# A two-layer encoder step on one core: the order in which weights are split, one last quarter instead of two halves, and two groups of moved work

## The chip, the cores and the metric

The kernel runs on one core of one Trainium2 chip. Its time is device microseconds (us) of one execution; the figure of a kernel is the median of its runs. Five engines work side by side, each in the order of its own queue: TensorE (PE in the profile; PEld is its weight load), VectorE (DVE), ScalarE (ACT), GpSimd (POOL), and SyncE (SP), which here only starts DMAs.

## What is computed

One inference step of a small encoder for two request groups: a prompt of 1024 columns and 32 new columns of another stream, so T = 1056 columns of D = 1024. Layer A mixes with an mLSTM recurrence, layer B with windowed attention whose keys and values are shared; each is followed by a SwiGLU feed-forward (D_FF = 2816), and each of the four sub-layers by a LayerNorm of `alpha * x + sublayer(x)`. All of it is float32.

```
def trunk(x, ...):
    for layer in range(DEPTH):                       # DEPTH = 2
        if layer < N_A_LAYERS:
            mix, C, n, m = mlstm_mixer(x, w_in_a[layer], ..., w_out_a[layer], C0s[layer], n0s[layer], m0s[layer])
        else:
            if layer == N_A_LAYERS:
                kv = (x @ w_kv).reshape(B, T, 2, N_KV_HEADS, HEAD_DIM)
            mix = swa_prompt(...) if k_cache is None else swa_sample(...)   # window 128, sinks, ALiBi
        x = layer_norm(DEEPNORM_ALPHA * x + mix, ln_g[layer, 0], ln_b[layer, 0])
        x = layer_norm(DEEPNORM_ALPHA * x + swiglu(x, w_gu[layer], w_down[layer]), ln_g[layer, 1], ln_b[layer, 1])
    return x, jnp.stack(Cs), jnp.stack(ns), jnp.stack(ms), k_sh, v_sh

def swiglu(x, w_gu, w_down):
    g, u = jnp.split(x @ w_gu, 2, axis=-1)
    return (jax.nn.silu(g) * u) @ w_down
```

The outputs are the final x of both groups, the recurrent states, and the new rows of keys and values.

## The kernel before

**Products.** Every float32 product is made of three: a number is split into a high part `h` and a rest `l`, and TensorE adds h·h, h·l and l·h (`gemm`, L344 to L346, one line each). The columns are worked through in groups of 384, 384, 288 for projections and in quarters of 264 for everything else. Activations lie in `ACT`, their halves in `SX`.

**Weights.** Weights come from memory as float32 "units" of 128 x 1024 (`Weights`). `load_to` starts a unit's DMA into one of RAW = 3 buffers `wr` (queue of SyncE). `_next` splits the next half unit: the high part is a copy on ACT (L190), the rest a subtraction on POOL, or on DVE for the keys in `on_vector` (L192). The results lie in one of SLOTS = 5 pairs of buffers `wh`/`wl`, or in a place of their own (`home`: the tiles `ex` and `oh`). Feed-forward units come in pairs and give seven factors, some of them sums made on DVE. `get` and `factor` split what is missing at the place of use; `done` frees a unit's buffers and then splits on, until four slots are taken or the next unit is twelve or more ahead.

**The order of the work.** No scheduler moves instructions: each engine gets them in the order in which the program writes them. What is written when is set by `Weave`. It holds generators ("tasks": mLSTM, LayerNorm, staging, attention); `gemm` calls `tick` after each of its steps with the model time of three matmuls, 3 · (n/2400 + 0.003) us, n at least 256, and each task whose pause has run out writes its next instructions. The numbers in `LN_PACE` and after `yield` are such pauses. They aren't times of the chip.

**Stages, in time** (us of the profiled execution): loading and first projections (0 to 65); mLSTM beside the projections of q, k, v and the output gate (65 to 415); layer A's output projection, with LayerNorm (415 to 535); feed-forward of layer A: two plain tiles for each half of the columns (to 590), 20 up tiles in pairs with seven factors (to 1000), down blocks, and a last part in quarters (to 1250); keys, values, queries and attention (to 1530); layer B's output projection (to 1590) and feed-forward (plain tiles to 1675, up tiles to 2085, down to 2344); the last LayerNorm and the output (to 2357.5).

**Names that the change touches.**
- `proj_o` (L858 ff.) makes the output gate of one tile of 128 rows: L864, L866, L867 on ACT, L865, L868, L869, L871 on DVE. Behind it `split_act` (L374 on ACT, L375 on DVE) splits the activations for layer A's output projection, whose results L944 adds on DVE.
- `up_tile` makes one paired up tile: bank A of PSUM gets factor a1, ACT copies it out (L1128), bank B gets a2, and then bank A gets s2 on top. TensorE can't write that before L1128 has read the bank. Later copies are L1136 and L1143; L1155, in the generator `rest`, takes what bank A holds at the tile's end, and `finish_tile` writes it in the next tile.
- `stage(p)` brings the finished tiles 2p and 2p+1 to memory as operands of the down product: `put` copies a sum to a high part on ACT (L1016), subtracts on POOL or DVE (L1017) and starts a DMA on SyncE. Ahead of the first put, DVE makes two differences (L1028, L1029).
- `norm_tail` runs a product by quarters and starts a task `ln_task` for each: column means with TensorE (L406), L411 on DVE, squares L413 on ACT, their sums L415, the variance with TensorE (L420), L425 to L427 on ACT, L429 and L430 on DVE, then for pairs of tiles L433 on DVE and the gains L441 on ACT or L439 on DVE, and in the last feed-forward the output's DMA (L445). L469 sums the tiles for the mean. L1306 adds the down product's last part. In the last feed-forward the fourth quarter is worked in two pieces of 132 columns (`FINAL`).
- `k_part` (L1340 to L1344) and `v_parts` (L1387, L1388) split keys and values for attention. The cached ones (`ck`, `cv`) are done ahead of attention's start. In attention, L1456 and L1457 are scores, L1462 adds the bias and takes a minimum (DVE), L1474 is the exponential, L1480 (POOL) the division.

## Time and profile before

| | |
|---|---|
| median of 3 runs | 2361.19 us (2358.27 to 2363.21) |
| the profiled execution, its own time | 2360.58 us |
| its span, first to last instruction | 2357.5 us |
| granted clock of TensorE, mean | 0.985 |
| moved from and to memory | 289.73 MB, mean 123 GB/s |

By stages of the span, TensorE's busy share and the granted clock:

| us | stage | PE busy us | clock |
|---|---|---|---|
| 65 to 355 | mLSTM beside projections | 271.13 of 290 | 0.98 |
| 355 to 415 | output gate | 60.00 of 60 | 1.00 |
| 415 to 535 | layer A's output projection | 109.86 of 120 | 0.94 |
| 535 to 590 | plain up tiles, layer A | 51.77 of 55 | 1.00 |
| 1000 to 1250 | down, layer A | 246.13 of 250 | 1.00 |
| 1250 to 1530 | keys, values, queries, attention | 250.10 of 280 | 0.96 |
| 1675 to 2085 | up tiles, layer B | 403.31 of 410 | 1.00 |
| 2085 to 2344 | down, layer B | 255.35 of 259 | 0.99 |

How to read it: times of single instructions are nanoseconds where marked, else us. A row of a timeline is start, duration, engine, line, operation, what is written and read, shapes, and in brackets the idle time ahead of it with what ended it. A duration of a matmul in such a row is longer than the distance to the next one, since matmuls overlap; distances are taken from counts and busy time.

### The profile page before, as it was taken

Reading aid. Unit: us, or ns where it says so; the run is one execution under the profiler, and the core shown is the slowest. Engines: PE = TensorE matmul, PEld = TensorE weight load, DVE = VectorE, ACT = ScalarE, POOL = GpSimd, SP = SyncE. Lnnn points to the kernel's source line nnn. Section 1 sums busy time; section 2 is a strip of 40 time slices with the busy share of each in tenths; the row PEclk is TensorE's granted clock in tenths of the full one; section 3 lists DMA queues with packets and bytes.
Section 4 is the critical chain, followed back from the end, with each engine's and each line's share of the span. In section 5 each row is a group of like instructions: output and inputs, shape, how many; then the busy total and the mean of one; then the engine's idle time right before and its main releaser. Section 6 shows DMA issues by size and latency. Waiting matters only on the chain. (4 is left out here: it accounts for less than half of the span.)

```text
span 2357.5 us, 44628 instructions
## 1 busy us (share of the span) xinstructions
PE 2246.9 (95%) x17370; PEld 2190.0 (93%) x17370; DVE 1459.9 (62%) x2772; ACT 1026.3 (44%) x2313; POOL 1114.8 (47%) x1038
## 2 busy tenths in 40 slices
PE   8999989899999999999998899899999999999997
PEld 8888979899999999999998799899999999999997
DVE  4354456668556556466667677777755555556655
ACT  3343345355444344322247677746444444322133
POOL 1443333325566556554314676723665565554410
PEclk9999999899999999999999999999999999999999
DMA  4222111301343334597423110331343344396711
GB/s 141 61 61 51 54 41 55 127 19 57 144 146 142 142 130 154 198 329 241 157 84 107 54 50 27 108 104 54 110 154 130 137 146 147 128 356 227 231 57 56
DMA packets 166179, 289.73 MB, mean 123 GB/s; under 512 B 15888, under 2 KB 121928, under 8 KB 165968
## 3 DMA queue, kind: packets, MB, share of 16 engines
q1 hardware_dynamic: 161616, 282.56, 36.0%
q10 hardware_dynamic: 4352, 4.33, 0.5%
q8 instruction: 136, 2.23, 0.4%
q14 instruction: 75, 0.61, 0.1%
HBM read 203.89 MB, written 82.94 MB: 122 GB/s over the span
## 5 line engine op out<-in xcount | busy, mean ns | idle before, releaser
L192 POOL TENSOR_TENSOR wl_s<-wr,wh_s 128x512 fp32r<-128x512 f32 x224 | 315.2, 1427 | 303.0 <-ACT wh_s L190 230.7
L344 PE MATMUL d<-sx,wh 128*128 128x264 f32 (+3 forms) x1092 | 350.0, 321 | 12.8 <-ACT sx L374 8.7
L346 PE MATMUL d<-sx,wl 128*128 128x264 f32 (+3 forms) x1092 | 335.4, 307 | 7.6 <-POOL wl L192 7.6
L345 PE MATMUL d<-sx,wh 128*128 128x264 f32 (+3 forms) x1092 | 334.6, 306 | 0.7 <-DVE sx L375 0.7
L190 ACT CAST wh_s<-wr 128x512 fp32r<-128x512 f32 x224 | 135.5, 617 | 332.3 <-DVE wr L167 300.7
L344 PE MATMUL A<-sx,wh_s 128*128 128x264 f32 x896 | 254.9, 284 | 2.8 <-ACT z L1143 2.8
L345 PE MATMUL A<-sx,wh_s 128*128 128x264 f32 x896 | 254.2, 284 | 0.0
L346 PE MATMUL A<-sx,wl_s 128*128 128x264 f32 x896 | 254.0, 283 | 0.0
L192 POOL TENSOR_TENSOR wl<-wr,wh 128x512 fp32r<-128x512 f32 (+2 forms) x108 | 143.2, 1345 | 183.4 <-ACT wh L190 178.5
L344 PEld LDWEIGHTS d<-sx,wh 128*128 128x128 f32 x1092 | 208.6, 191 | 18.5 <-ACT sx L374 9.4
L346 PEld LDWEIGHTS d<-sx,wl 128*128 128x128 f32 x1092 | 207.9, 190 | 10.2 <-POOL wl L192 10.2
L345 PEld LDWEIGHTS d<-sx,wh 128*128 128x128 f32 x1092 | 208.6, 191 | 2.4 <-DVE sx L375 1.6
L344 PE MATMUL d<-sx,ex 128*128 128x264 f32 (+1 forms) x660 | 192.5, 292 | 8.7 <-DVE act L944 5.0
L346 PE MATMUL d<-sx,ex 128*128 128x264 f32 (+1 forms) x660 | 189.1, 286 | 3.3 <-DVE ex L192 3.3
L345 PE MATMUL d<-sx,ex 128*128 128x264 f32 (+1 forms) x660 | 188.8, 286 | 0.0
L192 POOL TENSOR_TENSOR wl_a<-wr,wh_a 128x512 fp32r<-128x512 f32 x112 | 156.5, 1405 | 47.4 <-ACT wh_a L190 47.4
L344 PEld LDWEIGHTS A<-sx,wh_s 128*128 128x128 f32 x896 | 168.4, 188 | 3.6 <-ACT z L1143 3.6
L346 PEld LDWEIGHTS A<-sx,wl_s 128*128 128x128 f32 x896 | 168.9, 188 | 0.0
L345 PEld LDWEIGHTS A<-sx,wh_s 128*128 128x128 f32 x896 | 168.4, 188 | 0.0
L1480 POOL TENSOR_SCALAR s<-s,st 128x256 f32<-128x256 f32 (+1 forms) x144 | 122.5, 863 | 63.0 <-DVE st L1478 39.8
L1017 POOL TENSOR_TENSOR z<-z 128x528 fp32r<-128x528 f32 x76 | 111.2, 1463 | 67.7 <-ACT z L1016 67.4
L344 PE MATMUL A<-ex,wh_s 128*128 128x264 f32 x448 | 129.7, 289 | 9.4 <-ACT z L1128 9.4
(281 smaller groups left out, 7360.3 us busy)
## 6 DMA issues: line engine op xcount, KB each, us to landing
wr<-in_gu SPq DMA_DIRECT2D x96, 512.0 KB
hs_x<-z SPq DMA_DIRECT2D x72, 528.0 KB
hs_t<-z SPq DMA_DIRECT2D x64, 528.0 KB
sx<-hs_x SPq DMA_DIRECT2D x112, 264.0 KB
sx<-hs_t SPq DMA_DIRECT2D x64, 264.0 KB
ex<-hs_t SPq DMA_DIRECT2D x64, 264.0 KB
wr<-in_dn SPq DMA_DIRECT2D x32, 512.0 KB
ex<-hs_x SPq DMA_DIRECT2D x32, 264.0 KB
```

Source lines behind the costliest of these rows:

```text
L190: self.nc.scalar.copy(hi, r)
L192: eng.tensor_sub(lo, r, hi.bitcast(F32))
L344: nc.tensor.matmul(out, ah, bh, start=start and k == 0, stop=False, **kw)
L345: nc.tensor.matmul(out, ah, bl, start=False, stop=False, **kw)
L346: nc.tensor.matmul(out, al, bh, start=False, stop=stop and k == last, **kw)
L1017: eng.tensor_sub(lo.bitcast(F32R), buf(s), hi)
L1480: nc.gpsimd.tensor_scalar_mul(p[:R, h, lo:256], p[:R, h, lo:256], st[:R, 2, h : h + 1])
```

## The change

1. Splits by a clock. `Weave.tick` now also calls `W.feed`. While `W.ahead` is set, `feed` splits one half unit (or factor) whenever FEED_W = 1.7 us of model time have gone by since the last, into all five slots, and `done` splits nothing. While it isn't set, `done` splits on until four slots are taken, with no limit on how far ahead. `ahead` is set from the end of the first q and k projections to the paired up tiles of layer A, and from the end of a layer's down blocks to the next paired up tiles. Calls that split ahead by hand are gone (in `proj_v`, and the list `early` behind `proj_o`), and the second halves of layer A's output units go to DVE.
2. `FINAL` is gone: the last quarter of the last feed-forward is one piece of 264 columns.
3. `stage(p)` is started in the next even tile, behind that tile's first copy (before: from `rest` of the odd tile, so ahead of that copy), and for the last pair behind the last tile.
4. The cached keys and values are split behind the keys and values of the prompt, which run beside attention's start.
5. Two paces: the last quarter's LayerNorm in odd sub-layers (4.0 to 3.4 and 1.2 to 0.9), and `other_parts`, the splits of activations ahead of layer A's output projection (0.6 to 1.2).

```diff
+FEED_W = 1.7
-    ((2.4, 0.9, 0.9, 2.8, 0.8, 1.2, 0.6), (2.8, 0.7, 0.8, 4.0, 0.8, 1.4, 1.2)),
+    ((2.4, 0.9, 0.9, 2.8, 0.8, 1.2, 0.6), (2.8, 0.7, 0.8, 3.4, 0.8, 1.4, 0.9)),
...
     def tick(self, us):
+        if self.feed:
+            self.feed(us)
         for t in list(self.tasks):
...
-        while len(self.live) < SLOTS - 1 and self.njob < len(self.jobs) and self.jobs[self.njob][0] - u < 12:
-            if not self._next():
-                break
+        while not self.ahead and len(self.live) < SLOTS - 1 and self.njob < len(self.jobs) and self._next():
+            pass
+
+    def feed(self, us):
+
+        self.wait -= us
+        if self.ahead and self.wait <= 0 and self._next():
+            self.wait = FEED_W
...
-    on_vector.update((u, 1) for u in U_OUT_B[1])
+    on_vector.update((u, 1) for u in U_OUT_A[0] + U_OUT_B[1])
...
-    FINAL = [*QUARTERS[:3], quarter(3, 0, N4 // 2), quarter(3, N4 // 2, N4 // 2)]
+    QUARTERS = [(group(g), (g % 2, slice(0, N4))) for g in range(4)]
...
-        groups = FINAL if final else QUARTERS
-        for g, (cols, (c, zs)) in enumerate(groups):
+        for g, (cols, (c, zs)) in enumerate(QUARTERS):
...
-            if j and c in (2, 5):
-                W.factor((*U_Q, U_O[0])[j + 1], c // 5)
...
             gtask = wv.launch(gate_task())
+            W.ahead = True
...
-            for _ in range(2):
-                W.factor(*early.pop(0))
...
                 split_act(k, g)
-                yield 0.6
+                yield 1.2
...
             nc.scalar.copy(gate0, a)
+            if i > FIRST and not i % 2:
+                staging.append(wv.launch(stage(i // 2 - 1)))
...
-                if i % 2:
-                    staging.append(wv.launch(stage(i // 2)))
...
+        W.ahead = False
         px.pool = {o: px.enter_context(pool("ps" + o, PSUM)) for o in "BA"}
...
         finish_tile()
+        staging.append(wv.launch(stage(FT // 2 - 1)))
...
         px.close()
+        W.ahead = True
         dense_psum(6)
...
-    v_parts(9, cv[:], P)
-    k_part(ck, SEQ, P)
-    cx.close()
...
         keys_values(g)
         wv.launch(v_turn(g))
+    v_parts(9, cv[:], P)
+    k_part(ck, SEQ, P)
```

Lines of the changed kernel are some 2 to 12 higher: L190 and L192 become L196 and L198, L374 and L375 L386 and L387, L864 L870, L944 L947, L1016 L1019, L1128 L1131, L1155 L1160, L1388 L1392, L1462 L1463. What the change moves is seen in the order of three queues.

**ACT at the turn from an odd up tile to an even one, layer A.** `A` is PSUM's bank A, `wh` a weight's high part, `z` a buffer of the staging area. Before:

```order
L1155 ACTIVATE z_634_4638<-A_701_6754 128x528
L1016 CAST z_634_4638<-z_634_4638 128x528
L190 CAST wh44_s1_7022<-wr45_6849 128x512
L1128 COPY z_634_4638<-A_705_6989 128x528
```

Now:

```order
L1148 COPY z_634_4632<-A_697_6514 128x528
L196 CAST wh42_b2_6713<-wr43_6618 128x512
L1019 CAST z_634_4632<-z_634_4632 128x528
L196 CAST wh42_s2_6750<-wr43_6618 128x512
L1160 ACTIVATE z_634_4632<-A_697_6514 128x528
L196 CAST wh42_s1_6782<-wr43_6618 128x512
L1131 COPY z_634_4632<-A_701_6754 128x528
L1019 CAST z_634_4632<-z_634_4632 128x528
```

The gate's copy out of bank A has come ahead of the first put's copy L1019 (before L1016); one weight split stays between.

**ACT at the end of the output gate and the start of layer A's output projection.** `d` is a PSUM bank, `ex` and `wh` take split weights, L374 (now L386) splits activations. Before:

```order
L190 CAST ex_633_4634<-wr28_4716 128x512 x2
L190 CAST ex_633_4634<-wr29_4771 128x512 x2
L190 CAST wh30_0_4855<-wr30_4809 128x512
L190 CAST wh30_1_4859<-wr30_4809 128x512
L864 ACTIVATE z_634_4638<-d_640_4865 128x288
L866 ACTIVATE z_634_4638<-z_634_4638 128x288
L867 ACTIVATE z_634_4638<-z_634_4638 128x288
L190 CAST wh31_0_4897<-wr31_4847 128x512
L190 CAST wh31_1_4901<-wr31_4847 128x512
L374 CAST sx_76<-act_75 128x384 x8
L374 CAST sx_76<-act_75 128x288 x8
```

Now:

```order
L196 CAST ex_633_4628<-wr28_4737 128x512
L196 CAST ex_633_4628<-wr29_4775 128x512
L870 ACTIVATE z_634_4632<-d_640_4845 128x288
L872 ACTIVATE z_634_4632<-z_634_4632 128x288
L873 ACTIVATE z_634_4632<-z_634_4632 128x288
L386 CAST sx_76<-act_75 128x384 x2
L196 CAST ex_633_4628<-wr29_4775 128x512
L386 CAST sx_76<-act_75 128x384 x2
L196 CAST wh30_0_4934<-wr30_4813 128x512
L386 CAST sx_76<-act_75 128x384
```

Six splits stood ahead of the last L864, now two stand ahead of L870; the others have gone in between the splits of activations.

**DVE at attention's start.** `Q` are queries, `KL` and `VR` rests of keys and values, `psS` scores, `ck` and `cv` the cached rows. Before:

```order
L1372 SCALAR_TENSOR_TENSOR Q_895_14264<-d_894_14235,Q_895_14264 64x384
L1388 TENSOR_TENSOR VR_13973<-cv_880_13979,VR_13973 128x2x64
L1342 TENSOR_TENSOR KL0_13971<-ck_879_13977,KH0_13969 64x128
L1344 CAST KL0_13971<-KL0_13971 64x128
L1342 TENSOR_TENSOR KL1_13972<-ck_879_13977,KH1_13970 64x128
L1344 CAST KL1_13972<-KL1_13972 64x128
L1388 TENSOR_TENSOR VR_13973<-O_897_14302,VR_13973 128x2x64
L1462 ISA s_900_14316,st_901_14317<-psS0_13967,bt_882_13982 128x129
```

Now:

```order
L1375 SCALAR_TENSOR_TENSOR Q_895_14265<-d_894_14230,Q_895_14265 64x384
L1378 SCALAR_TENSOR_TENSOR Q_895_14265<-d_894_14230,Q_895_14265 64x384
L1392 TENSOR_TENSOR VR_13977<-O_897_14288,VR_13977 128x2x64
L1463 ISA s_900_14302,st_901_14303<-psS0_13971,bt_882_13983 128x129
L1463 ISA st_901_14303 128x1
```

The five instructions on cached rows have left the place between the last query and the first scores.

More of the change, by code (lines that the diff above doesn't have):

```diff
@@ L67, in __init__ @@
         self.tasks = []
+        self.feed = None
     def launch(self, gen):
@@ L131, in __init__ @@
         self.jobs, self.last = [], {}
+        self.wait, self.ahead = 0.0, False
         u = 0
@@ L297 @@
     add_ffn(1)
-    on_vector.update((u, 1) for u in U_OUT_B[1])
+    on_vector.update((u, 1) for u in U_OUT_A[0] + U_OUT_B[1])
     on_vector.update((u, f) for u in U_Q[:1] + U_KV[0] + U_QB[0][:1] for f in range(2))
     W = Weights(nc, base, units, pairs, on_vector)
+    wv.feed = W.feed
     ident = base.tile([P, P], F32, name="ident")
@@ L379, in group @@
         return slice(g * N4, (g + 1) * N4)
-    def quarter(g, a=0, n=N4):
-        return slice(g * N4 + a, g * N4 + a + n), (g % 2, slice(a, a + n))
-    QUARTERS = [quarter(g) for g in range(4)]
-    FINAL = [*QUARTERS[:3], quarter(3, 0, N4 // 2), quarter(3, N4 // 2, N4 // 2)]
+    QUARTERS = [(group(g), (g % 2, slice(0, N4))) for g in range(4)]
     def ln_task(z_, lps, grp, li, last, final):
@@ L474, in norm_tail @@
             last = g >= 3
-            tasks.append(wv.launch(ln_task(box[0].z, box[0].lnps, groups[g], li, last, final)))
+            tasks.append(wv.launch(ln_task(box[0].z, box[0].lnps, QUARTERS[g], li, last, final)))
         return tasks
@@ L905, in scratch @@
         return zz[:, 2 * i, :n], zz[:, 2 * i + 1, :n]
-    early = [(u, f) for u in U_OUT_A[0][:6] for f in range(2)]
     for g in range(3):
@@ L1374, in q_group @@
         )
-    cx = ExitStack()
-    pc = cx.enter_context(pool("pc", side="right"))
-    ck = new(pc, "ck", [P, P])
+    ck = new(pb, "ck", [P, P])
     nc.sync.dma_start(ck[:], A["cache_k"])
-    cv = new(pc, "cv", [P, P])
+    cv = new(pb, "cv", [P, P])
     kout = new(pb, "kout", [P, P + DEC])
```

## The prediction

> **What bounds the kernel now.** First the head of the page: who is busy, and how busy.
>
> ```profile
> span 2357.5 us, 44628 instructions
> PE 2246.9 (95%) x17370; PEld 2190.0 (93%) x17370; DVE 1459.9 (62%) x2772; ACT 1026.3 (44%) x2313; POOL 1114.8 (47%) x1038
> ```
>
> TensorE is busy in all but 2357.5 − 2246.9 = 110.6 us. So time can come from two places only: fewer or faster matmuls, and these 110.6 us. Next, the waits of TensorE, added up by what ended them; columns: total us, times, longest us.
>
> ```profile
> PE A L344 <- ACT z L1128: 9.4, 14, 1.8
> PE T L742 <- DVE act L790: 8.7, 4, 3.9
> ...
> PE psS L1456 <- DVE st L1462: 8.7, 4, 5.1
> PE d L346 <- POOL wl L192: 7.6, 10, 0.9
> ...
> PE d L344 <- DVE act L944: 5.0, 1, 5.0
> ...
> PE d L344 <- ACT z L864: 3.7, 1, 3.7
> ...
> PE d L344 <- ACT wh L190: 3.0, 4, 1.8
> ```
>
> No engine is the culprit throughout: TensorE waits for single results of ACT, DVE and POOL, whose own busy shares are 44 to 62%. These are questions of order in their queues. Third, windows by stage; columns: length, then busy us and count for PE, PEld, DVE, ACT, POOL, then granted clock, DMA share, GB/s.
>
> ```profile
> 110.00:355.00 245.00, 229.83 (x1635) 208.53 (x1635) 125.11 (x509) 101.27 (x364) 93.38 (x182) 0.98 0.21 51
> 425.00:430.00 5.00, 4.06 (x18) 4.06 (x19) 3.02 (x4) 2.36 (x7) 5.00 (x4) 0.50 0.43 117
> 435.00:440.00 5.00, 3.43 (x15) 3.43 (x16) 5.00 (x13) 1.53 (x5) 0.00 (x0) 0.50 0.49 121
> 590.00:1000.00 410.00, 403.81 (x3296) 401.91 (x3295) 235.25 (x259) 166.66 (x301) 242.83 (x174) 1.00 0.42 150
> 1280.00:1285.00 5.00, 3.93 (x16) 3.80 (x17) 2.50 (x15) 2.13 (x9) 1.26 (x3) 0.53 0.56 166
> 2310.00:2344.00 34.00, 33.55 (x293) 33.15 (x292) 18.57 (x47) 12.79 (x27) 1.32 (x1) 1.00 0.17 57
> ```
>
> Two things show. The up tiles (590 to 1000) run at 403.81 / 3296 = 0.1225 us a matmul of 264 columns, and the last quarter, cut into pieces of 132, at 33.55 / 293 = 0.1145. Half the columns save 7%. And behind the long waits (3.7 and 5.0 at 422 to 437, 5.1 at 1276 to 1281) the clock is 0.50 to 0.53: part of the busy time there is a further price of the wait, which the sum of the waits doesn't contain.
>
> **Part 1: the last quarter in one piece.** The two pieces are 8 tiles × 6 steps × 3 = 144 matmuls each. Before: 288 × 0.1145 = 33.0 us. After: 144 × 0.1225 = 17.6. TensorE ends 15.4 us earlier. The tail behind the last matmul pays for it, since its LayerNorm now has 264 columns. The same line at both widths (x528 are two rows of 264, x264 two of 132; columns behind the count: busy us, mean ns), and then the first step of the tail.
>
> ```profile
> L411 DVE TENSOR_TENSOR act<-ln,act 128x528 f32<-128x528 f32 x12 | 8.0, 701 | 3.7 <-PE ln L406 3.7
> ...
> L411 DVE TENSOR_TENSOR act<-ln,act 128x264 f32<-128x264 f32 x8 | 3.1, 424 | 1.2 <-PE ln L406 1.2
> ```
>
> ```profile
> 2343.59 0.29 DVE L1306 TENSOR_TENSOR act<-act,d 128x132 f32<-128x132 f32 x1
> ```
>
> From 2343.59 to the end of the span are 13.9 us. A wide pair costs 0.28 us more (0.70 against 0.42). The chain has one L469, four L411, three sums L415 and four L433, all of this shape: 12 × 0.28 = 3.4. Of the other 13.9 − 12 × 0.42 = 8.9 us (L1306, the two groups of LayerNorm matmuls, three activations, L429, L430, the gains L439, the output transfers and their landing) I let some 4 grow by the same ratio, 0.66, +2.4 rounded down; a transfer's landing and the steps between engines don't grow. Tail +5.8, net **−9.6** (−7 to −12; the ends are a tail of +8.4, where nearly all of it grows, and of +3.4, the pairs alone). What could eat it is the third quarter's LayerNorm: it now has 17.6 us to be emitted in, not 33. In the program's order its last apply L433 stands ahead of the final L469, so the tail is left clean.
>
> The Trainium skill, page "TensorE: Matmul & The Clock Gate", section "Back-to-back issue gap", gives N/2.4 + 2.5 ns a matmul: 57.5 ns at 132 columns and 112.5 at 264. By that, two half pieces cost what one whole costs, this part would gain 0.4 us on TensorE and lose 5.8 in the tail. The 0.1145 measured here speaks against it; the same page's weight load, 128/1.2 = 107 ns whatever N, agrees with the trace.
>
> **Part 2: staging behind the gate's copy.** One of the 14 waits for L1128, on ACT:
>
> ```profile
> 673.37 0.64 ACT L1016 CAST z<-z 128x528 fp32r<-128x528 f32 x1 [2.93 <-DVE z L1029]
> 673.91 0.62 ACT L190 CAST wh_s<-wr 128x512 fp32r<-128x512 f32 x1
> 674.43 0.59 ACT L1128 COPY z<-A 128x528 f32<-128x528 f32 x1
> ```
>
> L1016 is the first put of a staged pair. It waits for two DVE subtractions, and L1128, which TensorE needs, stands behind it in ACT's queue. After, the copy stands ahead of L1016. All 14 waits are in even tiles behind this launch (7 in each layer), so **−9.4**, their whole sum. Nothing late comes next: ACT idles 2.93 us here. Ends: 0, if the puts, now up to a copy's place later, fall ahead of another copy that TensorE needs; −11.7, if the slower first matmul behind each wait goes too (my estimate, 0.17 us × 14).
>
> **Part 3: splits dealt out.** Each unit costs two L190 and two L192. Their number is unchanged; only their place moves. Four places gain.
>
> *The start of layer A's output projection*, ACT then DVE then POOL:
>
> ```profile
> 422.38 2.16 ACT L190 CAST ex<-wr 128x512 fp32r<-128x512 f32 x4
> 424.45 1.13 ACT L190 CAST wh<-wr 128x512 fp32r<-128x512 f32 x2
> 425.49 0.40 ACT L864 ACTIVATE z<-d 128x288 f32<-128x288 f32 x1
> ```
> ```profile
> 423.00 0.46 DVE L869 SCALAR_TENSOR_TENSOR z<-z 128x288 f32<-128x288 f32 x1
> ...
> 427.72 1.42 DVE L869 SCALAR_TENSOR_TENSOR z<-z 128x288 f32<-128x288 f32 x1
> 429.17 1.42 DVE L871 SCALAR_TENSOR_TENSOR act<-act,gn,z 128x288 f32<-128x288 f32 x1
> 431.00 5.17 DVE L375 TENSOR_TENSOR sx<-act,sx 128x384 fp32r<-128x384 f32 x5 [0.41 <-ACT sx L374]
> ```
> ```profile
> 423.06 5.76 POOL L192 TENSOR_TENSOR ex<-wr,ex 128x512 fp32r<-128x512 f32 x4 [2.17 <-ACT ex L190]
> ```
>
> Six splits (3.2 us) stand ahead of L864, on which TensorE waited 3.7; after, two. That takes 2.2 off the wait. A wait of 1.5 is no longer than the 1.8 of L1128, and the window with those has clock 1.00; so half of the 4.06 us at half clock goes too: −4.2 together. The second wait, 5.0, ends when L944 comes up behind five L375; after, three L375 and one split: 1.03 × 2 less, 0.7 to 1.4 more, −1. And L869 and L871 take 1.42 beside POOL's burst, 0.46 without: with POOL's share halved I take three of them at 0.46, −2.9. Sum **−8**; ends −1 (one stall merely turns into the other) and −12.4 (both waits, 8.7, and the clock's 3.7).
>
> The page "SBUF — State Buffer", section "SBUF: two separate sides", says that DVE and GpSimd share a port pair by an exclusive lock, held for a whole instruction. Against this change it would say that the six splits newly put on DVE are blocked by POOL's: 6 × (1.42 − 0.46) = 5.8 us on DVE, by which this −8 would be −2. The rows above show such blocking, yet with fewer POOL splits there is also less to be blocked by.
>
> *mLSTM*, POOL:
>
> ```profile
> 148.99 4.96 POOL L192 TENSOR_TENSOR wl<-wr,wh 128x512 fp32r<-128x512 f32 x4 [1.31 <-ACT wh L190]
> ...
> 228.72 4.97 POOL L192 TENSOR_TENSOR wl<-wr,wh 128x512 fp32r<-128x512 f32 x4 [1.31 <-ACT wh L190]
> ```
>
> Behind such a burst of four, POOL's next mLSTM step comes 4.96 us late, and TensorE's longest wait for L790 is 3.9. Dealt out, a step has one split ahead of it, 3.7 less. These are the two bursts; some groups of four remain in the program's order. I take 2.5 a burst: **−5** (0 to −9; the whole window idles 245 − 229.8 = 15.2).
>
> *Half units ready one step sooner.* The ten waits for wl are 0.9 or less, each for the first half of a unit whose halves were split together; dealt out, the first half is a whole L190 (0.54) and L192 (1.24) earlier: **−5** (0 to −7.6).
>
> *Attention's start.* The wait for wh is 1.8 at its longest, there; fed sooner, −1.4. Then cached keys.
>
> ```profile
> 1276.44 1.00 DVE L1388 TENSOR_TENSOR VR<-cv,VR 128x128 fp32r<-128x128 f32 x1 [0.24 <-ACT VR L1387]
> 1277.36 1.34 DVE L1342 TENSOR_TENSOR KL<-ck,KH 64x128 fp32r<-64x128 f32 x1
> ...
> 1280.72 0.28 DVE L1462 CUSTOM_DVE_ANT_0 s<-psS,bt 128x129 f32<-128x129 f32 x1
> ```
>
> From 1276.44 to 1280.52 DVE does cached values and keys, with the first L1462 behind them and TensorE waiting 5.1. They go behind the keys of the prompt: −4.0, and of the clock at 0.53 behind it 3.93 × 0.47 = −1.8; +0.7 where they come back beside attention, on a DVE that is then full. **−6.5** with the wh (−2 to −9).
>
> **Part 4: what it may cost.** FEED_W is one half per 1.7 us of model time and fills all five slots. Splits now fall into LayerNorm's and mLSTM's chains of ACT and POOL at places where none stood, and puts come later by a fraction of a tile. The trace shows no such place. Nearest is the mean wait for L1128, 9.4 / 14 = 0.67; I take eight of them, **+5** (−2, since POOL's pairs in attention are broken up too, to +15). LN_PACE, 0.6 → 1.2 and the dropped `early` calls only re-order and stand in these terms.
>
> Sum: −9.6 − 9.4 − 8 − 5 − 5 − 6.5 + 5 = −38.5. The profiled execution took 2360.58 (span 2357.5 and 3.1 around it), 0.6 below the median 2361.19. 2360.6 − 38.5 = **2322**.
>
> **Rivals.** *A: as summed*, 2305 to 2340; chance 0.60. *B: the waits only move.* ACT, DVE and POOL work in order; a split taken from one chain falls into the next, and a wait that loses its first cause ends on its second. Then only part 1 and half of part 2 hold: −14 to −17, 2345. For it speaks that 15.2 us idle in the mLSTM window spread over several releasers; against it, that ACT idles 2.93 right ahead of L1016. 0.21. *C: the issue-gap rule* would hold for the halved pieces: 2322 + 15 = 2337; the 0.1145 is against it. 0.03. *D: the deal starves TensorE.* While it runs, finishing a unit splits no successor; a unit used faster than 2 × 1.7 = 3.4 us of model time is split at its use, with TensorE standing. The output projection's first quarter uses a unit per 8 × 0.34 = 2.7. Price: L190 plus L192, 0.54 + 1.24 = 1.8 us a unit, with the clock behind. It decides from 38.5 / 1.8, some 21 late units of about 80 that are dealt; with 30, 2322 + 54 = 2376. Against it: six units of layer A's projection have homes of their own and are split ahead. 0.09 for over 0.2%, 0.07 for ending within it. The measurement of this kernel tells some 0.2% (4.7 us) from no change.
>
> **Numbers.** A, B and C end faster by over 0.2%: 0.84; D gives same 0.07, slower 0.09. The range takes A with the ends of its terms and B: 2300 to 2347, near 0.82.
>
> **What would show it.** Part 1: some 144 fewer PE rows, the last 144 matmuls at 0.12, a tail of 19 to 20 us. Part 2: the row for L1128 gone from TensorE's waits, and no new row over 3 us from the up tiles. Part 3: clock above 0.9 in the stretch before layer A's projection and at attention's start; L944 and L1462 waits under 2; mLSTM idle near 10. If waits for wh and wl grow beyond their 3.0 and 7.6, D is at work; if they fall and others rise by as much, B.

## The result, and the profile after

The changed kernel takes **2308.07 us** (median of 4 runs, 2306.47 to 2310.11), the one before 2362.20 (4 runs, 2358.27 to 2364.76): 54 us less, a ratio of 0.9773 (95% interval 0.9756 to 0.9790). The forecast was 2322, within 2300 to 2347. The profiled execution took 2310.11 with a span of 2308.3, against 2360.58 and 2357.5: the two traces account for 49.2 us. One execution of the runs further down, 2421.55 us at a mean granted clock of 0.845, was a slow one and is left out of its run's figures.

The head of the page:

```profile
span 2308.3 us, 44279 instructions
PE 2216.2 (96%) x17218; PEld 2164.3 (94%) x17218; DVE 1458.4 (63%) x2752; ACT 1025.0 (44%) x2302; POOL 1118.5 (48%) x1030
```

TensorE is idle 92.1 us instead of 110.6, and busy 30.7 less. The other engines' busy times are those of before within 4 us. TensorE's waits by what ended them (total us, times, longest us):

```profile
PE ln L414 <- DVE z L476: 7.9, 10, 1.9
PE ln L428 <- DVE z L423: 7.7, 3, 4.9
...
PE psS L1457 <- DVE st L1463: 5.5, 3, 3.1
...
PE d L356 <- DVE act L947: 4.8, 1, 4.8
PE d L358 <- DVE ex L198: 3.4, 5, 1.2
PE d L357 <- POOL sx L461: 3.4, 2, 1.7
...
PE d L358 <- DVE wl L198: 3.0, 2, 1.5
PE T L747 <- DVE act L795: 2.9, 5, 1.2
...
PE d L358 <- POOL wl L198: 1.2, 2, 0.7
```

Compare row by row. The 9.4 us on the gate's copy (L1128, now L1131) have no row any more. The wait for DVE's L790 (now L795) fell from 8.7 to 2.9, with the longest 1.2 instead of 3.9. The wait for POOL's `wl` fell from 7.6 to 1.2, but 3.4 on POOL's L461 and 3.0 for `wl` from DVE's L198 are new. L944 (now L947) has lost only 0.2, and the longest wait of a variance, L428 in the tail, has grown from 3.5 to 4.9. Windows of the changed kernel:

```profile
65.00:355.00 290.00, 276.15 (x1956) 253.18 (x1953) 145.59 (x553) 118.09 (x411) 117.65 (x214) 0.99 0.20 56
590.00:1000.00 410.00, 407.10 (x3351) 406.68 (x3350) 245.92 (x270) 167.13 (x300) 250.85 (x176) 1.00 0.47 167
1675.00:2085.00 410.00, 408.59 (x3363) 408.19 (x3363) 250.22 (x274) 162.80 (x292) 249.39 (x176) 1.00 0.50 174
...
2269.00:2287.00 18.00, 18.00 (x143) 17.71 (x141) 11.14 (x21) 6.58 (x13) 1.32 (x1) 1.00 0.14 48
```

The up tiles idle 2.9 and 1.4 us in 410, where they idled 6.2 and 6.7. The last of these windows lies inside the last quarter: 143 matmuls in 18.0 us without idle time, 0.126 each, a few of them LayerNorm's. The quarter itself runs from 2267.7 to 2287.2, 19.5 us; before, its two pieces ran from 2308.6 to 2343.6, 34.9 us. The tail behind it, as a timeline of the changed kernel (start us, us, engine, line, what):

```profile
2287.75 0.42 DVE L1312 TENSOR_TENSOR act<-act,d 128x264 f32<-128x264 f32 x1
...
2289.06 1.85 PE L414 MATMUL ln<-z,onesm 128*128 128x264 f32 x4 [1.87 <-DVE z L476]
2290.95 2.55 DVE L419 TENSOR_TENSOR act<-ln,act 128x528 f32<-128x528 f32 x4 [2.04 <-PE ln L414]
...
2293.42 2.32 DVE L423 TENSOR_TENSOR z<-z 128x528 f32<-128x528 f32 x3
...
2295.80 2.13 PE L428 MATMUL ln<-z,onesm 128*128 128x264 f32 x4 [4.88 <-DVE z L423]
```

From L1312 to the end of the span are 20.6 us, against 13.9.

**By place.** Both programs use the weights' units in the same order. So the starts of the first matmuls that read a given unit, taken from the two traces, cut the run into the same pieces:

| from the first matmul of ... to the next row | before, starts at us | after, starts at us | gained in the piece |
|---|---|---|---|
| (start of the span) | 0 | 0 | 2.4 |
| second q unit (mLSTM begins beside it) | 66.3 | 63.9 | 5.9 |
| seventh tile of the output gate | 390.2 | 381.9 | 6.9 |
| seventh tile of layer A's output projection | 444.8 | 429.6 | 0.5 |
| second half of the plain up tiles, layer A | 553.7 | 538.0 | 0.9 |
| second paired up tile | 602.3 | 585.7 | 8.1 |
| down blocks | 999.4 | 974.8 | 0.1 |
| queries, attention | 1253.1 | 1228.3 | 9.3 |
| layer B's output projection | 1483.7 | 1449.6 | −3.1 |
| plain up tiles, layer B | 1612.2 | 1581.2 | 1.1 |
| second paired up tile | 1686.9 | 1654.8 | 6.7 |
| down blocks, first three quarters of the last part, last quarter | 2082.7 | 2043.9 | 17.6 |
| last matmul of the down product, then the tail | 2343.3 | 2286.9 | −7.2 |

These are pairs of single executions. Between runs whose programs don't differ there, the mLSTM stretch came out 5.5 us apart (313.6 to 319.1), layer B's output projection 3.5 us apart (128.8 to 132.3), the other stretches up to layer B's down blocks within 1.5. So the −3.1 in layer B's output projection is not shown to be a loss: runs with the splits in bursts took 128.5 to 131.3 there.

### The profile page after: what moved, and what is told of

It reads as the page before. It is cut to its first block, busy times and chain, and to the rows that moved or that the text cites. A ratio compares the mean times of both kernels' runs of the same rounds, so it can differ in the third digit from the quotient of the medians.

```text
span 2308.3 us, 44279 instructions
## 1 busy us (share of the span) xinstructions
PE 2216.2 (96%) x17218; PEld 2164.3 (94%) x17218; DVE 1458.4 (63%) x2752; ACT 1025.0 (44%) x2302; POOL 1118.5 (48%) x1030
## 4 chain that ended last, share of the span: by engine, by line
PE 77%; DVE 9%; ACT 7%; DMA 3%; issue 3%; POOL 1%; SPq 0%; DVEq 0%; ACTq 0%; POOLq 0%
PE A L356 9%; PE A L358 9%; PE A L357 9%; PE d L356 8%; PE d L358 8%; PE d L357 8%; PE B L356 7%; PE B L357 7%; PE B L358 7%; ACT act L449 1%; PE T L1501 1%; DVE z L476 1%; PE psS L1457 1%; DVE act L441 1%; ACT wh L196 1%
## 5 line engine op out<-in xcount | busy, mean ns | idle before, releaser
L198 POOL TENSOR_TENSOR wl_s<-wr,wh_s 128x512 fp32r<-128x512 f32 x224 | 316.8, 1434 | 238.9 <-ACT wh_s L196 179.3
L356 PE MATMUL d<-sx,wh 128*128 128x264 f32 (+2 forms) x1080 | 347.2, 321 | 8.5 <-ACT sx L386 7.5
L357 PE MATMUL d<-sx,wh 128*128 128x264 f32 (+2 forms) x1080 | 332.7, 308 | 4.4 <-POOL sx L461 3.4
L358 PE MATMUL d<-sx,wl 128*128 128x264 f32 (+2 forms) x1080 | 332.1, 307 | 4.2 <-DVE wl L198 3.0
L196 ACT CAST wh_s<-wr 128x512 fp32r<-128x512 f32 x224 | 135.3, 617 | 316.7 <-DVE wr L173 289.0
L198 POOL TENSOR_TENSOR wl<-wr,wh 128x512 fp32r<-128x512 f32 (+2 forms) x106 | 144.4, 1370 | 220.2 <-ACT wh L196 193.0
L198 POOL TENSOR_TENSOR wl_a<-wr,wh_a 128x512 fp32r<-128x512 f32 x112 | 170.2, 1526 | 51.3 <-ACT wh_a L196 42.2
L356 PE MATMUL d<-sx,ex 128*128 128x264 f32 x624 | 181.3, 291 | 4.9 <-DVE act L947 4.8
L358 PE MATMUL d<-sx,ex 128*128 128x264 f32 x624 | 178.3, 286 | 3.5 <-DVE ex L198 3.4
L357 PE MATMUL d<-sx,ex 128*128 128x264 f32 x624 | 177.8, 285 | 0.0
L1020 POOL TENSOR_TENSOR z<-z 128x528 fp32r<-128x528 f32 x76 | 105.0, 1382 | 103.9 <-issue 50.3
L1019 ACT CAST z<-z 128x528 fp32r<-128x528 f32 x136 | 85.9, 631 | 95.6 <-DVE z L1032 47.0
```

The lines of the kernel that those rows point to most:

```text
L196: self.nc.scalar.copy(hi, r)
L198: eng.tensor_sub(lo, r, hi.bitcast(F32))
L356: nc.tensor.matmul(out, ah, bh, start=start and k == 0, stop=False, **kw)
L357: nc.tensor.matmul(out, ah, bl, start=False, stop=False, **kw)
L358: nc.tensor.matmul(out, al, bh, start=False, stop=stop and k == last, **kw)
L1019: nc.scalar.copy(hi.bitcast(F32R), buf(s))
```

## The experiments

The executions of one changed program scatter by 3 to 9 us, and those of the kernel before by up to 12 within a series, so each effect is given by the medians beside 2308.07 (or that series' median of before), and where a place can be named, by the trace.

**Each part undone.** First the last quarter in two pieces again:

```diff
...
-        for g, (cols, (c, zs)) in enumerate(QUARTERS):
+        groups = FINAL if final else QUARTERS       # FINAL: the fourth quarter as 132 + 132 columns
+        for g, (cols, (c, zs)) in enumerate(groups):
...
```

> The changed kernel with only the last quarter of the last feed-forward cut into two pieces of 132 columns again. Theory (weight loads set the pace, so a half piece costs nearly a whole one): the changed kernel's profile shows the last 144 matmuls 15.6 us earlier and a tail 7 us longer, so this undoing loses 8 us: about 2316 against 2308. Rival 1 (matmul time goes with the columns): it gains some 6 us, 2302, since the tail alone gets shorter. Rival 2 (the longer tail eats all of it): 2308 to 2310.

2317.33 us (2312.96 to 2320.47), ratio to before 0.9799 (0.9772 to 0.9826): 9.3 slower by the medians, 6 by the ratios, since two of that series' seven runs of before lie 8 and 10 us above their median. In the trace, TensorE's last quarter is 15.4 us longer and the tail behind it 7.1 shorter, 8.3 together. The theory holds, and both rivals fall. A window of this run that holds the two pieces:

```profile
2262.00:2297.00 35.00, 35.00 (x308) 34.74 (x306) 19.63 (x48) 13.93 (x30) 1.32 (x1) 1.00 0.18 63
```

35.0 us for 308 matmuls (16 of them LayerNorm's), 0.114 each, without any idle time and at a granted clock of 1.00: the pieces aren't held up by anything, they cost what they cost.

Then the staging ahead of the gate's copy again:

```diff
-            if i > FIRST and not i % 2:
-                staging.append(wv.launch(stage(i // 2 - 1)))
...
                 yield 0.5
+                if i % 2:
+                    staging.append(wv.launch(stage(i // 2)))
...
-        staging.append(wv.launch(stage(FT // 2 - 1)))
```

> The changed kernel with only the staging started from the end of the odd tile again, ahead of the even tile's first copy. Theory (the waits were made by this order alone): the 14 waits on the gate's copy come back with their 9.4 us, 11.7 us by distances between matmuls; about 2319. Rival (part of the gain in the up tiles comes from the dealt splits, which stand elsewhere now): 5 us or less, 2313.

2322.01 us (2319.83 to 2322.37), ratio 0.9819 (0.9794 to 0.9843): 13.9 slower. The waits are back to the tenth:

```profile
PE A L356 <- ACT z L1131: 9.4, 14, 1.8
```

By starts of units the two stretches of up tiles lose 5.7 and 7.5 us, 13.2, and the one behind layer B's 2.6 more. So the order alone made these waits, and their price was above even the forecast's far end of 11.7.

Then the splits as before:

```diff
-        while not self.ahead and len(self.live) < SLOTS - 1 and ... and self._next():
+        while len(self.live) < SLOTS - 1 and ... and self.jobs[self.njob][0] - u < 12:
...
-    wv.feed = W.feed
...
-    on_vector.update((u, 1) for u in U_OUT_A[0] + U_OUT_B[1])
+    on_vector.update((u, 1) for u in U_OUT_B[1])
...
+                W.factor((*U_Q, U_O[0])[j + 1], c // 5)
...
+                W.factor(*early.pop(0))
...
-                yield 1.2
+                yield 0.6
```

> The changed kernel with the splits as before: no feed, refill at done with the limit of twelve, the early calls, second halves of layer A's output units on POOL, pace 0.6 for the splits of activations. Theory (bursts of splits held up ACT and POOL): loses what the forecast gave to part 3 without the cached keys, 8 + 5 + 5 + 1.4 = 19 us, about 2327, with TensorE's waits on L790's successor and on the gate's last activation back at 8 and 4 us. Rival (waits only move): 5 us or less, 2313. Second rival (the dealt splits gave more than forecast, which is why the whole came out 15 us better): 25 us or more, 2333.

2337.02 us (2335.69 to 2341.04), ratio 0.9887 (0.9861 to 0.9913): 29 slower. The second rival is right: the dealt splits gave more than half of the whole. The waits that the expectation named are back, the first of them longer than before:

```profile
PE T L749 <- DVE act L797: 13.4, 7, 5.1
...
PE d L356 <- ACT z L872: 3.7, 1, 3.7
```

And the cached keys first again:

```diff
...
         wv.drain(t)
+    v_parts(9, cv[:], P)
+    k_part(ck, SEQ, P)
...
-    v_parts(9, cv[:], P)
-    k_part(ck, SEQ, P)
```

> The changed kernel with only the cached keys and values split ahead of attention's start again. Theory: TensorE's wait for the first scores goes from 3.1 back to 5 or more and the clock behind it stays low longer: loses 4 to 6 us, about 2313. Rival (the start of attention is held by other work of DVE as well, and the cached keys fill time that would be idle): 1 us or less, 2308 to 2309.

2308.58 us (2307.86 to 2311.67), ratio 0.9763 (0.9733 to 0.9792): 0.5 slower, no difference that these runs resolve, so the 4 to 6 us of the theory did not come. Its wait did: the longest for the first scores is 5.5 where the changed kernel has 3.1, and the stretch of attention is 1.7 us longer (table further down).

```profile
PE psS L1462 <- DVE st L1468: 8.0, 3, 5.5
```

DVE in this run:

```profile
1253.27 0.32 DVE L1394 TENSOR_TENSOR VR<-cv,VR 128x128 fp32r<-128x128 f32 x1
1253.51 0.27 DVE L1348 TENSOR_TENSOR KL<-ck,KH 64x128 fp32r<-64x128 f32 x1
...
1254.39 1.23 DVE L1350 CAST KL<-KL 64x128 fp32r<-64x128 f32 x1
...
1255.86 0.28 DVE L1468 CUSTOM_DVE_ANT_0 s<-psS,bt 128x129 f32<-128x129 f32 x1
```

The same five instructions stand ahead of the first scores and take 2.4 us, not the 4.0 of before: `VR` 0.32 instead of 1.00, the first `KL` 0.27 instead of 1.34. Before, POOL worked beside them, at that very time:

```profile
1275.99 1.30 POOL L453 TENSOR_TENSOR sx<-act,sx 128x528 fp32r<-128x528 f32 x1
1277.25 2.58 POOL L192 TENSOR_TENSOR wl<-wr,wh 128x512 fp32r<-128x512 f32 x2
```

The Trainium skill's page "SBUF — State Buffer", section "SBUF: two separate sides", has a rule for it: DVE and GpSimd exclude each other from a shared port pair for a whole instruction. The durations above fit it: in both kernels the long ones end within some 0.2 us of a POOL subtraction's end.

The four undoings add up to 9.3 + 13.9 + 29 + 0.5 = 52.7 of 54 us by the medians. By the ratios they add up to some 42, and by the spans of the profiled executions to 45. So most of the gain is found part by part; how much lies in the parts' interplay these runs don't tell, but one case is shown below.

**The feed beside mLSTM alone**, put into the kernel before:

```diff
...
+    wv.feed = W.feed
...
             gtask = wv.launch(gate_task())
+            W.ahead = True
...
-            if j and c in (2, 5):
-                W.factor((*U_Q, U_O[0])[j + 1], c // 5)
...
+    W.ahead = False
     def proj_o(m, g, release):
```

> The kernel before with one part alone: splits dealt out by the feed while mLSTM runs (from the first projections to the last q, k, v tile), refill at done as before afterwards, the two factor calls of the values' projection dropped. Theory (undoing all splits cost 29 us, and some 15 of these lay between 65 and 324 us): this alone brings 12 to 16 us, about 2348 against 2362, and TensorE's wait for the mLSTM state's placing on DVE (L790, 8.7 before) falls to some 3. Rival (the forecast's size, two bursts of 2.5 each): 5 us, 2357, the wait falling to some 4. Second rival (the stage differs from execution to execution by as much): no difference of the medians.

2349.47 us (2346.55 to 2352.47) against 2363.36, ratio 0.9932 (0.9909 to 0.9955): 13.9 faster. The theory holds, and the forecast's 5 falls. Its wait and its window, then the same window of the kernel before:

```profile
PE T L753 <- DVE act L801: 2.2, 5, 0.8
```

```profile
65.00:355.00 290.00, 277.70 (x1990) 253.97 (x1988) 146.37 (x558) 120.75 (x417) 115.49 (x216) 1.00 0.21 56
```

```profile
65.00:355.00 290.00, 271.13 (x1920) 247.05 (x1918) 136.80 (x545) 116.85 (x407) 113.42 (x215) 0.98 0.21 54
```

1990 matmuls got through in the time of 1920. TensorE idles 12.3 us instead of 18.9, and the clock is 1.00 instead of 0.98, which is 0.02 × 271 = some 5 us more. So nearly half of what this pair gains is the clock. That share isn't the same in every execution: with the same deal, this window's clock was 0.99 in the changed kernel and 0.98 in the run with the splits of activations later. Where it was lost is seen in the kernel before, behind the first of the two bursts of POOL and the wait of 3.9:

```profile
156.00:160.00 4.00, 4.00 (x18) 3.97 (x18) 1.69 (x8) 2.74 (x10) 1.47 (x4) 0.71 0.64 211
160.00:164.00 4.00, 4.00 (x27) 3.78 (x25) 0.93 (x4) 0.69 (x2) 1.99 (x5) 1.00 0.08 23
```

The stretch varies between executions: up to the output gate's seventh tile, the three profiles in which splits come in bursts took 390.2, 392.4 and 397.3 us (before, the run with the cached keys moved alone, and the undone splits), those in which they are dealt at 1.7 took 378.4 to 384.5 (ten profiles). The two sets don't overlap; their means lie 12 us apart. The pair of traces in the table, 390.2 and 381.9, is the fastest of the one set and one from the upper half of the other, which is most of why the traces account for 49 us and the medians for 54.

**The feed half as fast:**

```diff
-FEED_W = 1.7
+FEED_W = 3.4
```

> The changed kernel with one half unit per 3.4 us of model time instead of 1.7. Theory (rival D of the forecast: a unit that is used faster than it is dealt is split at its use, 1.8 us of ACT and POOL with TensorE standing): 15 to 30 units late, 2335 to 2360, with TensorE's waits for wh and wl at 20 us or more. Rival (five slots and the split at the next use hide it): 2308 to 2315.

2325.41 us (2322.51 to 2327.08), ratio 0.9826 (0.9800 to 0.9852): 17 slower, between theory and rival.

```profile
PE d L356 <- ACT wh L196: 7.2, 5, 2.3
...
PE d L358 <- DVE ex L198: 4.8, 5, 2.1
...
PE d L358 <- POOL wl L198: 3.8, 6, 0.8
```

Waits for `wh`, which the changed kernel hasn't, are 7.2; all waits for weight splits together 18.0, against 7.6 there. So a slow deal does starve TensorE, as rival D of the forecast said, but the waits for `wh` and `wl` are 12 us and not the 20 expected, and it's still faster than the bursts.

**Layer A's output units on POOL:**

```diff
-    on_vector.update((u, 1) for u in U_OUT_A[0] + U_OUT_B[1])
+    on_vector.update((u, 1) for u in U_OUT_B[1])
```

> The changed kernel with the second halves of layer A's eight output units split on POOL again, all else dealt out. Theory (with the bursts gone it matters little which engine takes them; DVE loses six splits of 0.7 and pays for it where POOL runs beside it): 0 to 3 us slower, 2308 to 2311. Rival (two-input work of DVE is blocked while POOL works, so the move to DVE cost time): 3 us or more faster, 2305. Second rival (the move to DVE carries the gain at the output projection's start): 5 us or more slower, 2313.

2309.77 us (median of three, 2305.45 to 2313.65; ratio 0.9763, 0.9734 to 0.9792): no difference is shown. In the trace the wait on L947 is longer than the changed kernel's 4.8:

```profile
PE d L356 <- DVE act L947: 6.7, 1, 6.7
```

and the stretch from the output gate's seventh tile to the projection's seventh takes 50.2 us instead of 47.7. So the move to DVE helped there by some 2.5 us, by this trace. The forecast had weighed the port rule as a price of that move; no such price is seen.

**The splits of activations later:**

```diff
     def other_parts():
+        yield 2.8
         for g in range(1, 3):
...
-                yield 1.2
+                yield 1.1
```

> The changed kernel with the splits of activations ahead of layer A's output projection begun 2.8 us of model time later, 1.1 apart instead of 1.2, so that DVE's first addition L947 stands ahead of them instead of behind three. Theory (the wait of 4.8 us there is L947's place in DVE's queue): the wait falls to under 2, the clock behind it stays up, 3 to 5 us faster, 2303 to 2305. Rival (the wait ends on something else that DVE has to do first, the gate's last multiplications): 1 us or less, 2307 to 2308.

2304.67 us (2303.30 to 2306.34), ratio 0.9743 (0.9721 to 0.9764). Its wait (L948 here), then the window around it for the changed kernel and for this one:

```profile
PE d L356 <- DVE act L948: 2.4, 1, 2.4
```

```profile
415.00:440.00 25.00, 20.16 (x150) 19.81 (x149) 20.23 (x37) 10.07 (x24) 5.07 (x4) 0.93 0.59 196
```

```profile
415.00:440.00 25.00, 22.62 (x180) 22.11 (x179) 21.52 (x40) 11.28 (x27) 6.51 (x4) 1.00 0.58 193
```

The wait halves and the clock stays at 1.00: the stretch takes 43.5 us instead of 47.7, 4.2 less, and the medians say 3.4. The wait was in good part L947's place in DVE's queue, and less than half of what that cost was the clock behind it: 2.4 us less waiting, 4.2 us gained. It fell to 2.4, not under 2 as expected: what DVE does just ahead of L948 now is the gate's last product and one weight split, which is the part that the rival named.

**The cached keys alone**, in the kernel before:

```diff
...
         wv.drain(t)
-    v_parts(9, cv[:], P)
-    k_part(ck, SEQ, P)
...
         wv.launch(v_turn(g))
+    v_parts(9, cv[:], P)
+    k_part(ck, SEQ, P)
```

> The kernel before with one part alone: cached keys and values split behind those of the prompt. The undoing of this part in the changed kernel cost 0.5 us; there the splits are dealt out. Theory (the 4.0 us that this work took on DVE before were made by POOL's burst of splits beside it, so either of the two changes is enough): alone it brings 4 to 6 us, 2357 against 2362, and TensorE's wait for L1462 falls from 5.1 to 3 or less. Rival (the place never mattered, other work of DVE ends the wait): 0 to 1 us, the longest wait stays at 5.

2362.44 us against 2364.61, ratio 0.9994 (0.9983 to 1.0006): not told from no change; the interval allows a gain of up to 4 us, the lower end of the 4 to 6 expected. At the place itself the wait falls as the theory said; it is 1.39 where it was 5.11:

```profile
1279.87 0.58 PE L1451 MATMUL psS<-KH,Q 128*128 128x256 f32 x1 [1.39 <-DVE st L1457]
```

The stretch from the first queries to layer B's projection shows the two causes apart (us, by starts of units):

| | cached keys first | moved |
|---|---|---|
| splits in bursts there | 230.6, 230.3 | 227.6, 226.6, 228.0 |
| splits dealt out | 222.9 | seven runs, 220.8 to 221.6 |

The cached keys are worth 3 us with bursts and 1.7 without; the deal 6 to 8. The medians of whole runs are too coarse to show the smaller two: this is the interplay, and it rests on the traces.

**No feed around attention:**

```diff
         px.close()
-        W.ahead = True
         dense_psum(6)
```

> The changed kernel in which the feed isn't switched on again after the down blocks, so that from there (last part of the down product, attention, layer B's output projection, plain tiles of layer B) units are split when others are done, as outside the dense work. Theory (some 8 of the 29 us of the dealt splits lie there, mostly in attention, where POOL's pairs of splits stood ahead of its division L1481): 5 to 10 us slower, 2313 to 2318, lost between attention's start and layer B's plain tiles. Rival (waits only move in attention, and mLSTM with the first output projection, 14 and 7 us, is all there is): 0 to 2 us.

2316.92 us (2312.81 to 2318.31), ratio 0.9784 (0.9768 to 0.9800), where the changed kernel had 0.9773: 8.9 slower by the medians, 3 by the ratios, whose before ran slower in this series; the intervals of the two ratios overlap. The trace says 8, of which 6.7 in attention (the 228.0 of the table). POOL's division, which the expectation named, is in the row

```profile
PE T L1500 <- POOL s L1480: 3.5, 7, 1.0
```

only in small part (2.8 in the changed kernel). Two waits on DVE grew more, from 2.8 and from 0.2:

```profile
PE T L1500 <- DVE lo L1504: 5.6, 5, 2.4
...
PE O L1431 <- DVE VR L1391: 2.3, 1, 2.3
```

Why DVE is late there wasn't tried.

**The tail, and three waits less.** First matmuls that nobody reads, to keep the clock up:

```diff
...
+        if final and last:
+            warm(17)          # 17 matmuls of 264 columns into a spare bank
         yield y[0]
...
+        if final and last:
+            warm(36)
         yield y[1]
```

> The changed kernel with matmuls that nobody reads put into the two idle times of TensorE in the tail (17 ahead of the last mean, 36 ahead of the last variance); the outputs don't depend on them. Theory (the tail came out longer than forecast since its 4 + 4 LayerNorm matmuls ran at half clock behind an idle TensorE, 1.85 and 2.13 us, where those of other quarters took 1.05): they take 1.05 each and the tail gets 1.9 us shorter. Rival (they are slow because they wait for their operands one by one): they stay at 1.8 to 2.1.

A single execution: 2303.43 us, span 2301.6.

```profile
2283.84 1.11 PE L421 MATMUL ln<-z,onesm 128*128 128x264 f32 x4
2284.59 4.80 PE L399 MATMUL d<-sx 128*128 128x264 f32 x36
2289.83 1.16 PE L437 MATMUL ln<-z,onesm 128*128 128x264 f32 x4 [0.44 <-DVE z L432]
```

1.11 and 1.16 instead of 1.85 and 2.13. For the second group it is the clock, not the operands: it took 2.12 to 2.13 in every run with this tail and without the unread matmuls, and the theory holds. The first group's 1.85 was a matter of the single execution: in six of the eight such runs it took 1.13. From L1312 (L1321 here) to the end of the span the tail takes 19.1 us instead of 20.6; the other runs with the changed kernel's tail took 19.5 to 20.7, so the gain is 0.5 to 1.6.

Then this together with the later splits of activations, and the rests of the last quarter on DVE:

```diff
-                eng = nc.gpsimd if kk & 1 else nc.vector
+                eng = nc.gpsimd if kk & 1 and not (last and not li & 1) else nc.vector
```

> The changed kernel with three edits: the splits of activations later as in the run before, TensorE kept busy in the tail, and the last quarter's rest of the activations (L461, layer A's and layer B's output projection) all on DVE instead of half on POOL. Theory (the waits for wl in the plain up tiles did not go but moved to POOL's L461, 1.7 us in each layer): 3.7 + 1.9 + 3.4, 2299 to 2300, and the wait on POOL's L461 is gone. Rival (it moves once more, to DVE's splits): 2303.

2304.47 us (2299.03 to 2307.25), ratio 0.9740 (0.9722 to 0.9759), where 2299 to 2300 was expected; the profiled execution, with a span of 2297.2, is the fastest of the four. The wait on POOL's L461 is gone, and DVE's split has grown a little:

```profile
PE d L358 <- DVE wl L198: 3.5, 2, 1.8
```

Faster than the changed kernel, but from the run with the first of its three edits alone (0.9743) it can't be told by these medians. In the trace the three places gain 2.4, 2.3 in both layers' plain tiles together, and 1.5 in the tail.

## Why the prediction was right, point by point

**What bounds the kernel** held: TensorE, with fewer matmuls and shorter waits as the only sources, and the clock behind waits as part of their price. The forecast was 14 us too high all the same. That it lies inside the range is owed to the range's lower end, which let every term reach its best, and in part to luck, as terms too small and terms too large stand against each other below. Of its signs, these held: no row for L1128, no new row over 3 us in the up tiles, a clock of 0.93 at layer A's projection, mLSTM idle 10.8 of its 245 us. The tail was to be 19 to 20 us and is 20.6. The waits on L947 and L1463 were to be under 2 and are 4.8 and 3.1, and the clock at attention's start was to be above 0.9 and is 0.66:

```profile
1250.00:1260.00 10.00, 7.10 (x33) 6.78 (x34) 4.67 (x22) 5.81 (x21) 7.01 (x10) 0.66 0.50 165
```

**Part 1, forecast −9.6.** The traces give 15.4 us earlier and a tail 7.2 longer, −8.2; undoing it cost 9.3. The step with an error is the 2.4 for the rest of the tail: the two groups of LayerNorm matmuls took 1.85 and 2.13 us, not a share of 4 us grown by the columns (the second at half clock, the first longer in this execution than in most), and two L441 of the third quarter still stood ahead of the last L1312 in DVE's queue (0.6 us), where the forecast had looked at the order against L469 alone. The gap rule for matmuls (rival C) is out for this kernel: 0.114 for 132 columns. The Trainium skill, page "TensorE: Matmul & The Clock Gate", section "Back-to-back issue gap", gives that formula for a single matmul and says that in a stream of weight loads and matmuls both set the spacing. So the formula isn't that section's rule for a stream like this one, and the 0.114 agrees with what it says of streams.

**Part 2, forecast −9.4.** 13.9 by undoing, 14.8 by the traces. Mechanism and number of waits exact; the size is short because the wait's own time was taken (0.67 each), not the time lost between the matmuls. Part of that is the clock. The forecast read a clock of 1.00 in the window with these waits and took a wait of up to 1.8 to be free of it; over 410 us one stretch at half clock is lost in the rounding. Before, behind one of the longest of the 14:

```profile
631.99 0.39 PE L344 MATMUL A<-ex,wh_s 128*128 128x264 f32 x1 [1.78 <-ACT z L1128]
```

```profile
632.80:636.20 3.40, 3.40 (x18) 3.40 (x17) 2.20 (x2) 1.59 (x3) 3.40 (x3) 0.50 0.39 159
```

**Part 3, output projection, forecast −8.** 6.9 by the table. The wait on L864 went entirely, with its clock; that on L944 lost only 0.2, not 3.9. It is earlier by as much as TensorE is, so TensorE waits as long as before. The run with the activations' splits later shows what was left there.

**Part 3, mLSTM, forecast −5: the term that was mis-sized most.** 13.9 alone, 12 by the means of the traces. The step that failed: "I take 2.5 a burst". The waits behind the bursts went as a whole (8.7 to 2.2 for L790), and the clock behind them, 0.71 for 4 us and 0.98 over the stretch, wasn't priced here, though it was at the output projection and at attention. The clock's part differs from execution to execution, as said there.

**Part 3, half units, forecast −5: wrong.** The plain tiles gained 2 us together. 7.6 us of waits for POOL's `wl` became 1.2, but L461 on POOL and L198 on DVE took their place with 3.4 and 3.0. Rival B was right at this one place; the step that failed is that nothing was named which is late next. The run with L461 on DVE confirms the first of the two.

**Attention's start, forecast −6.5.** The place gained 9.3, for another reason. The five instructions took 4.0 us mainly because POOL subtracted beside them; their own time is near 1.3 (0.32, twice 0.27 to 0.29, twice 0.22), so moving them is worth 1.7 to 3, and the deal brought the rest. The step that failed is that durations measured beside POOL's bursts were taken as the cost of the work, in a change that removes those bursts.

**Part 4, forecast +5.** No such cost is shown. New waits stand in the plain tiles (already counted), the −3.1 at layer B's output projection is within the scatter of that stretch, and the up tiles took no harm from the later puts.

So the sum of −38.5 was 16 short by the medians. By these figures it was some 9 short in mLSTM, 5 in part 2 and 3 at attention, and too large by 3 for the half units, by 1 each at the output projection and in part 1; the 5 charged in part 4 did not come. The figures are from different pairs of runs, each with its scatter, so that they match the 16 only roughly. The 2.4 us ahead of mLSTM in the table, for which no term stood, are not shown to belong to the change: there the second q unit began at 65.4 to 66.3 us with bursts and at 63.9 to 65.8 with the deal.

## What to carry to other kernels

When one engine is the bound, read its waits by what ended them, then ask of each cause what else stands in that queue: a burst of helper work can cost more than the wait behind it, since the clock may fall and instructions on the neighbouring engine get longer. An instruction's duration belongs to its neighbourhood; if the change alters what runs beside it, the old duration isn't its price. And for each wait that goes, name the next one at that place: two of the forecast's terms failed by not doing so.

## What the runs showed of the hardware

- A matmul of 132 columns takes 0.114 us (the last quarter in two pieces) and one of 264 0.1215 to 0.126 (up tiles and last quarter of the changed kernel), back to back with new weights each time.
- The granted clock goes to 0.5 for stretches of about 3.4 us or more behind waits of TensorE, and the length of the wait doesn't settle it: before, it was 0.50 from 632.8 to 636.2 us behind a wait of 1.78 (1.00 on either side), and 1.00 from 235.0 to 238.4 behind one of 3.04 (row below); the 2.4 of the run with the splits of activations later left it at 1.00. The Trainium skill, page "TensorE: Matmul & The Clock Gate", section "What's actually happening", gives about 3.4 us of idle or busy time for either change. The length of the stretch at half clock agrees with that; that a wait of 1.78 is followed by one does not, and there the measurement decides.

```profile
235.00:238.40 3.40, 3.40 (x25) 3.19 (x26) 1.27 (x7) 2.02 (x9) 1.89 (x5) 1.00 0.68 235
```

- A copy of 64 by 128 on DVE took 0.22 us, and 1.17 (before) to 1.23 (cached keys first again) beside a subtraction on POOL.
